# A hybrid attention layer on one core: the opening's transfers in order of use on one queue, and idle products fed from a constant

## The chip, the cores and the metric

The kernel runs on one core of a Trainium2 chip. The metric is device time in microseconds (us) of one execution. The kernel before took 1103.35 us, the median of three runs from 1103.25 to 1103.62.

## What is computed

One layer of a streaming encoder for 256 tokens of width 2048, all in float32:

```python
h = rms_norm(x, attn_norm)                       # x: (1, 256, 2048)
x = x + hybrid_mixer(h, w_in, ..., w_out)        # 8 heads of softmax attention with forget gates,
                                                 # 8 heads of stick-breaking attention
h = rms_norm(x, ffn_norm)
x = x + conv_ffn(h, w_up, conv_w, conv_b, w_down) # up, causal convolution of width 3, gate, down
```

The mixer begins with `proj = h @ w_in`, whose first 512 columns are the queries of four heads. Only the computation of those columns, the opening of the kernel, is touched by the change.

## The kernel before

**Splitting.** Products run on TensorE (PE) in a reduced-precision float32 form. To keep the precision, each operand is split in a high part (a cast) and a low part (the operand less its high part), and high x high, high x low and low x high are added up. So each piece of weights is loaded (`w_raw`), cast on ScalarE (ACT) or VectorE (DVE) to `w_hi`, and subtracted on DVE to `w_lo`; the activations are transposed on PE, scaled with the norm's weights `ga` on ACT to the high part of `hT` (L143) and subtracted on DVE to its low part (L146).

**The opening** (`opening`, L385) makes the first 512 columns. Its 2048 rows of weights are taken in eight chunks c = 0 to 7 of 256 rows (two k-tiles of 128). `load_x(k, n)` (L90) loads n k-tiles of x for both halves of the tokens, on SyncE's queue (SP): 256 KB for n = 2. `load_w(c)` (L391) loads a chunk, 512 KB, and `load_w(c, i)` its half i, 256 KB, by default on SP's queue; in the text w(c,i) and x(k,n). Two chunks share one `w_raw` buffer, and there are three buffers. `columns` (L126) transposes the norm's weights `prow` to `ga`. `split_w(c)` (L402) makes a chunk's high and low parts; for chunk 0 it also transposes x(0,2), and for chunk 1 it casts the two halves on DVE (L415) and transposes x(2,2). `multiply(c, i, n, high)` (L423) makes the products of a chunk: with `w_hi`, per k-tile two with the high and two with the low part of `hT`, one for each half of the tokens; with `w_lo`, two with the high part. `behind(c)` (L454) puts the transposes and splits of later chunks ahead of a chunk's products. `sums_of_squares` (L155) runs on ACT.

**What sets the order.** The opening is written with the order of PE, DVE, ACT and SP fixed by hand: each engine executes its instructions as they stand in the code. A transfer is issued by an instruction of SP or ACT, in that engine's order; the two have a queue each (q1 and q10 in the profile), and both feed the same 16 DMA engines. A scheduler gives each transfer one of eight semaphores in turn, so a transfer can wait for an earlier one's landing. The order of the issues before is L433 to L448: on SP x(0,2), w(0,0), x(2,2), w(1,1), x(4,2), w(2), x(6,2), w(3), and so on; on ACT the norm's weights, then, behind the load of the activation table, w(0,1) and w(1,0).

**Idle products.** While the first transfers are on the way, PE has nothing to do. `keep_busy(n)` (L379) puts n products of 128x128 by 128x256 bfloat16 in its order, whose result nobody reads: 14 ahead of `columns`, 4 behind the transposes of chunk 0. They read `zeros`, a tile that DVE fills at L371. The preamble of every program fills some constants on GpSimd (L1160), among them a bfloat16 1.0 in each partition.

Behind the opening stand the rest of the projection, the attention heads, the output projection and the feed-forward part. The order on PE is fixed by hand there too, and weights are loaded up to six steps ahead.

Of the kernel before, what the change touches and what calls it, by code (L numbers as in the profile page):

```python
# [14 lines left out]
P = 128  # L15
D = 2048
S = 256
NT = S // P
KT = D // P
# [26 lines left out]
def hybrid_layer(  # L46
# [19 lines left out]
    nc = tc.nc  # L66
    act, dve = nc.scalar, nc.vector
# [10 lines left out]
    def f32(t):  # L78
        return t.bitcast(F32)
# [4 lines left out]
    prow = const.tile([50, P], F32, name="prow")  # L84
# [5 lines left out]
    def load_x(k, n):  # L90
        nc.sync.dma_start(x2[:, :, k * P : (k + n) * P], xp[:, :, k * P : (k + n) * P])
# [29 lines left out]
    ga = const.tile([P, KT], F32, name="ga")  # L121
# [4 lines left out]
    def columns(dst, rows, n):  # L126
        pp = psb.tile([P, 512], F32, name="pp", tag="t")
        nc.tensor.transpose(pp[:, :n], rows, ident[:n, :n])
        dve.tensor_copy(dst, pp[:, :n])
# [3 lines left out]
    def transposed_split(k, g, n=2):  # L133

        ps = psb.tile([P, 2, S], F32, name="ps_x", tag="t")
        for j in range(n):
            for t in range(NT):
                nc.tensor.transpose(  # L138
                    ps[:, j, t * P : (t + 1) * P], xt[t][:, (k + j) * P : (k + j + 1) * P], ident
                )  # L140
        for j in range(n):
            i = k + j
            act.activation(hT[:, i, 0, :], ps[:, j, :], AF.Identity, scale=g[:, i : i + 1])  # L143
        for j in range(n):
            i = k + j
            dve.scalar_tensor_tensor(  # L146
                hT[:, i, 1, :], ps[:, j, :], g[:, i : i + 1], f32(hT[:, i, 0, :]),
                op0=ALU.mult, op1=ALU.subtract,
            )

    def sums_of_squares(ss, c, tiles=range(NT)):

        for t in tiles:
            junk = late.tile([P, 512], F32, name="junk", tag="raw", bufs=4)
            act.activation(junk, xt[t][:, c * 512 : (c + 1) * 512], AF.Square, accum_out=ss[:, t, c : c + 1])  # L155
# [62 lines left out]
    def rows_of(w, k0, n, c0, cols):  # L218
        return w[k0 * P : (k0 + n) * P, c0 : c0 + cols].rearrange("(k p) c -> p k c", p=P)
# [14 lines left out]
    def of_half(h, part, t):  # L234
        return h[:, part, t * P : (t + 1) * P]
# [51 lines left out]
    with ExitStack() as actx:  # L287

        at = actx.enter_context(tc.tile_pool(name="at", bufs=1))
# [77 lines left out]

        zeros = at.tile([P, S], mybir.dt.bfloat16, name="zeros")  # L370
        dve.memset(zeros, 0.0)  # L371
        nc.gpsimd.memset(ident, 0.0)
        nc.gpsimd.affine_select(
            ident, ident, pattern=[[-1, P]], base=0, channel_multiplier=1,
# [2 lines left out]
        idle = pss.tile([P, S], F32, name="idle", tag="s")  # L377

        def keep_busy(n):  # L379
            for _ in range(n):  # L380
                nc.tensor.matmul(idle, zeros[:, :P], zeros, start=True, stop=True)

        ss1 = const.tile([P, NT, 4], F32, name="ss1")

        def opening():  # L385

            acc = psa.tile([P, NT, 512], F32, name="acc", tag="acc")
            pairs = [[(0, 1), (1, 1)]] + [[(0, 2)]] * 7
            raws, parts = [], []

            def load_w(c, which=None, queue=nc.sync):  # L391

                if c == len(raws):
                    raw = wraw.tile([P, 2048], F32, name="w_raw", tag="w_raw")
                    raws.extend([raw[:, :1024], raw[:, 1024:]])
                for i, n in [(which, 1)] if which is not None else [(0, 2)]:
                    queue.dma_start(
                        raws[c][:, i * 512 : (i + n) * 512].rearrange("p (a b) -> p a b", a=n),
                        rows_of(wi, 2 * c + i, n, 0, 512),
                    )  # L400

            def split_w(c):  # L402
                hi = whi.tile([P, 2048], F32R, name="w_hi", tag="w_hi")
                lo = wlo.tile([P, 2048], F32R, name="w_lo", tag="w_lo")
                parts.append([t[:, :1024].rearrange("p (a b) -> p a b", a=2) for t in (hi, lo)])
                for i, n in pairs[c]:
                    cols = slice(i * 512, (i + n) * 512)
                    if c == i == 0:
                        dve.tensor_copy(hi[:, cols], raws[c][:, cols])
                        for k in range(2):  # L410
                            transposed_split(k, ga, 1)
                    elif c == 1:
                        for j in range(2):
                            half = slice(512 * j, 512 * (j + 1))
                            dve.tensor_copy(hi[:, half], raws[c][:, half])  # L415
                        transposed_split(2, ga)
                    else:
                        act.copy(hi[:, cols], raws[c][:, cols])
                    dve.tensor_tensor(
                        lo[:, cols], raws[c][:, cols], f32(hi[:, cols]), op=ALU.subtract  # L420
                    )

            def multiply(c, i, n, high):  # L423
                hi, lo = (p[:, i : i + n] for p in parts[c])
                order = [(j, l, hi) for j in range(n) for l in range(2)] if high else [(j, 0, lo) for j in range(n)]
                for m, (j, l, r) in enumerate(order):
                    for t in range(NT):
                        nc.tensor.matmul(  # L428
                            acc[:, t, :], of_half(hT[:, 2 * c + i + j], l, t), r[:, j, :],
                            start=high and c == i == m == 0, stop=not high and c == 7 and m == n - 1,  # L430
                        )

            load_x(0, 2)  # L433
            nc.scalar.dma_start(prow[:KT, :], attn_norm[0].rearrange("(n p) -> n p", p=P))
            act.preload_act_table_set("natural_log_exp_and_others")
            load_w(0, 0)
            load_w(0, 1, nc.scalar)
            load_x(2, 2)
            load_w(1, 0, nc.scalar)
            load_w(1, 1)  # L440
            load_x(4, 2)
            load_w(2)
            load_x(6, 2)
            load_w(3)
            load_x(8, 4)
            load_w(4)
            load_x(12, 4)
            load_w(5)  # L448
            keep_busy(14)
            columns(ga, prow[:KT, :], KT)  # L450
            split_w(0)
            keep_busy(4)

            def behind(c):  # L454
                if c:
                    transposed_split(2 * c + 2, ga)
                split_w(c + 1)

            multiply(0, 0, 1, True)
            multiply(0, 1, 1, True)  # L460
            behind(0)
            sums_of_squares(ss1, 0, [0])
            multiply(0, 0, 1, False)
            multiply(0, 1, 1, False)
            for c in range(1, 8):
                if c < 7:
                    behind(c)
                sums_of_squares(ss1, c // 2, [c % 2])
                if c == 2:
                    load_w(6)  # L470
                    load_w(7)
                multiply(c, 0, 2, True)
                multiply(c, 0, 2, False)
            return acc

        with tc.high_priority(offset=AHEAD), tc.manual_schedule(
            engines={mybir.EngineType.PE, mybir.EngineType.DVE, mybir.EngineType.Activation, mybir.EngineType.SP}
        ):
            acc_q0 = opening()
# [301 lines left out]
        for group in range(2):  # L781
# [3 lines left out]
            for c in range(4):  # L785
# [7 lines left out]
                if c == 0:  # L793
                    pg = psb.tile([P, NT], F32, name="pg", tag="t")
                    for t in range(NT):
                        nc.tensor.matmul(
                            pg[:, t : t + 1], ssq[group][:, t * P : (t + 1) * P], ones[:, 0:1],
                            start=t == 0, stop=t == NT - 1,
# [376 lines left out]
```

## Time and profile before

| | |
|---|---|
| runs, median (lowest to highest) | 1103.35 us (1103.25 to 1103.62) |
| the profiled execution | 1103.81 us |
| span, first to last instruction | 1102.0 us |
| busy: PE, DVE, ACT, GpSimd | 1096.5, 877.7, 701.9, 44.4 us |
| HBM read | 242.82 MB, 222 GB/s over the span |
| packets on q1 (SP), share of 16 DMA engines | 162458, 58.6% |
| packets on q10 (ACT), share | 320, 0.1% |

The profile is one execution, recorded by the hardware. PE are the matrix products, PEld the loads of their stationary operand, SPq and ACTq the issues of transfers by SP and ACT. A row of the timeline gives start and length in us, engine, line of the kernel, operation, what is written from what, shapes and count; in brackets how long the engine stood idle before it and what ended that. A chain of waits follows the end back to what each step waited for. "Landing" is when all of a transfer's bytes have been reported.

### The profile page before, as it was taken

What the parts mean: (1) busy time and instruction counts of PE and PEld (TensorE: products, weight loads), DVE (VectorE), ACT (ScalarE), POOL (GpSimd) and SP (SyncE); (2) the same over time, 40 slices, a digit from 0 to 9 for tenths busy, and PEclk for the clock granted to TensorE, in tenths of its full rate; (3) what the DMA queues carried; (4) which work ended last, traced back from release to release, by engine and by line L of the source; (5) the groups of instructions that cost most, each with busy time, mean ns of one, the idle gap of its engine ahead of it and who ended that gap; (6) DMA issues with size and microseconds to landing.
All of it is one profiled execution on the core that took longest, in us unless ns stands there. A gap on an engine that the chain in (4) does not pass through costs nothing.

```text
span 1102.0 us, 14826 instructions
## 1 busy us (share of the span) xinstructions
PE 1096.5 (99%) x5868; PEld 951.2 (86%) x5868; DVE 877.7 (80%) x941; ACT 701.9 (64%) x879; POOL 44.4 (4%) x46
## 2 busy tenths in 40 slices
PE   9999999999999999999999999999999999999998
PEld 7998888888888888888888888888888888888887
DVE  5655777975775677689889988889798889889896
ACT  6544556664653566677767776767676777677753
POOL 0000000000000000000000010100000010100010
PEclk9999999999999999999999999999999999999999
DMA  8776654576545396558989597986979689997985
GB/s 288 171 244 230 188 156 153 153 231 197 184 161 186 112 317 196 181 191 209 288 223 312 191 234 264 261 269 177 315 209 303 217 218 282 241 266 198 322 208 177
DMA packets 179407, 245.89 MB, mean 223 GB/s; under 512 B 4432, under 2 KB 119018, under 8 KB 179082
## 3 DMA queue, kind: packets, MB, share of 16 engines
q1 hardware_dynamic: 162458, 209.67, 58.6%
q0 software_dynamic: 16560, 34.75, 16.8%
q8 instruction: 46, 0.75, 0.3%
q10 hardware_dynamic: 320, 0.53, 0.1%
q14 instruction: 23, 0.19, 0.0%
HBM read 242.82 MB, written 2.11 MB: 222 GB/s over the span
## 4 chain that ended last, share of the span: by engine, by line
PE 99%; DMA 0%; DVE 0%; SPq 0%; issue 0%
PE pu L254 34%; PE acc L229 22%; PE pu L260 18%; PE bank_a L229 10%; PE bank_b L229 5%; PE bank_c L229 2%; PE acc L428 2%; PE acc L1053 1%; PE ps_x L138 1%; PE ps_o L593 1%; PE bank_a L1053 1%; PE ps_p L607 0%; DMA w_raw<-in_w_in_dram 0%; PE ps_o L594 0%; PE ps_h L307 0%; PE ps_s L522 0%
## 5 line engine op out<-in xcount | busy, mean ns | idle before, releaser
L208 DVE TENSOR_TENSOR w_lo<-w_raw,w_hi 128x2048 fp32r<-128x2048 f32 (+1 forms) x196 | 439.6, 2246 | 129.5 <-ACT w_hi L207 128.6
L207 ACT CAST w_hi<-w_raw 128x2048 fp32r<-128x2048 f32 (+1 forms) x196 | 367.3, 1877 | 235.9 <-PE acc L229 66.6
L254 PE MATMUL pu<-hT,w_hi 128*128 128x512 f32 x1664 | 394.0, 390 | 0.0
L254 PEld LDWEIGHTS pu<-hT,w_hi 128*128 128x128 f32 x1664 | 310.3, 188 | 63.2
L260 PEld LDWEIGHTS pu<-hT,w_lo 128*128 128x128 f32 x1664 | 211.9, 191 | 7.0
L260 PE MATMUL pu<-hT,w_lo 128*128 128x256 f32 x1664 | 215.1, 283 | 0.0
L229 PE MATMUL acc<-w_hi,hT 128*128 128x512 f32 (+1 forms) x576 | 124.5, 368 | 0.0
L229 PEld LDWEIGHTS acc<-w_hi,hT 128*128 128x128 f32 x576 | 101.5, 188 | 14.3
L207 ACT CAST w_hi<-w_sum 128x2048 fp32r<-128x2048 f32 x30 | 57.3, 1909 | 44.2 <-PE pu L254 36.6
L208 DVE TENSOR_TENSOR w_lo<-w_sum,w_hi 128x2048 fp32r<-128x2048 f32 x30 | 68.7, 2290 | 20.8 <-ACT w_hi L207 20.7
L870 ACT ACTIVATE tap<-up,ccol 128x256 f32<-128x256 f32 x176 | 74.6, 495 | 0.0
L229 PE MATMUL acc<-w_lo,hT 128*128 128x512 f32 (+1 forms) x288 | 64.6, 366 | 0.0
L229 PEld LDWEIGHTS acc<-w_lo,hT 128*128 128x128 f32 x288 | 51.6, 188 | 7.5
L975 POOL DMA_DIRECT2D w_sum<-in_w_down_dram x20 | 25.7, 1284 | 797.7 <-DVE w_lo L208 786.1
L229 PE MATMUL acc<-w_hi,oT 128*128 128x512 f32 x192 | 46.0, 392 | 0.0
L229 PEld LDWEIGHTS acc<-w_hi,oT 128*128 128x128 f32 x192 | 35.7, 188 | 7.3
L229 PE MATMUL bank_a<-w_hi,g 128*128 128x512 f32 x160 | 40.0, 392 | 0.0
L229 PE MATMUL bank_b<-w_hi,s 128*128 128x512 f32 x160 | 40.0, 392 | 0.0
L229 PE MATMUL bank_a<-w_hi,s 128*128 128x512 f32 x160 | 40.0, 392 | 0.0
L229 PEld LDWEIGHTS bank_b<-w_hi,s 128*128 128x128 f32 x160 | 28.9, 189 | 5.2
L229 PEld LDWEIGHTS bank_a<-w_hi,g 128*128 128x128 f32 x160 | 28.8, 189 | 5.3
L229 PEld LDWEIGHTS bank_a<-w_hi,s 128*128 128x128 f32 x160 | 28.9, 189 | 5.2
(211 smaller groups left out, 1068.7 us busy)
## 6 DMA issues: line engine op xcount, KB each, us to landing
w_raw<-in_w_up_dram SPq DMA_DIRECT2D x88, 1024.0 KB, 7.5
w_raw<-in_w_down_dram SPq DMA_DIRECT2D x44, 1024.0 KB, 6.4
w_raw<-in_w_in_dram SPq DMA_DIRECT2D x36, 1024.0 KB, 5.4
w_sum<-in_w_down_dram POOLq DMA_DIRECT2D x20, 1024.0 KB, 9.9
w_raw<-in_w_out_dram SPq DMA_DIRECT2D x16, 1024.0 KB, 5.1
w_raw<-in_w_down_dram POOLq DMA_DIRECT2D x10, 1024.0 KB, 14.9
w_raw<-in_w_in_dram SPq DMA_DIRECT2D x12, 688.0 KB, 4.2
w_raw<-in_w_in_dram SPq DMA_DIRECT2D x6, 512.0 KB, 6.8
```

Source lines behind the costliest of these rows:

```text
L138: nc.tensor.transpose(ps[:, j, t * P : (t + 1) * P], xt[t][:, (k + j) * P : (k + j + 1) * P], ident)
L207: act.copy(hi[:, :n], raw[:, :n])
L208: dve.tensor_tensor(lo[:, :n], raw[:, :n], f32(hi[:, :n]), op=ALU.subtract)
L229: nc.tensor.matmul(o, lhs(i, l, t), r[:, i, :], start=starts and j == 0, stop=stops and j == 3 * n - 1, skip_group_check=more,)
L254: nc.tensor.matmul(acc[:, j, :], hi[:, i, j * P : (j + 1) * P], hT[:, k].rearrange("p a b -> p (a b)"), start=k == 0, stop=low_first and k ...
L260: nc.tensor.matmul(acc[:, j, S:], lo[:, i, j * P : (j + 1) * P], hT[:, k, 0, :], start=False, stop=not low_first and k == KT - 1,)
L428: nc.tensor.matmul(acc[:, t, :], of_half(hT[:, 2 * c + i + j], l, t), r[:, j, :], start=high and c == i == m == 0, stop=not high and c == ...
L593: nc.tensor.matmul(po, v[j][:, hs], wp[:, k], start=i == 0, stop=False)
L870: act.activation(taps[w][:, j, :], u[:, j, w : w + S], AF.Copy, scale=ccol[:, w, f : f + 1])
L975: nc.gpsimd.dma_start(mem[into][:, : nk * 512].rearrange("p (a b) -> p a b", a=nk), src, accum_op=ALU.add)
L1053: nc.tensor.matmul(o, of_half(g, l, t), r[:, i, c0 : c0 + cols], start=kh == 0 and j == 0, stop=kh == n - 1 and j == 11,)
```

## The change

The tile `zeros` and its memset go; the idle products read a view `some` of the preamble's 1.0, each partition's one element repeated (step 0). On SP's queue stand x and the first weights in the order in which they are used: x(0,2), w(0,0), w(0,1), x(2,2), w(1,0), x(4,2), w(1,1), x(6,2). ACT issues the norm's weights at the start, as before, and no longer w(0,1) and w(1,0); w(2) is now issued by ACT, and stands there behind the splitting of chunk 0 (two activations of L143 and a cast of L418). The other loads keep their order on SP. There are 16 idle products ahead of `columns`, for 14, and 3 behind the transposes of chunk 0, for 4.

```diff
-        zeros = at.tile([P, S], mybir.dt.bfloat16, name="zeros")
-        dve.memset(zeros, 0.0)
+        some = nc.const_aps.tensor(1.0, [P, S], mybir.dt.bfloat16)
...
         def keep_busy(n):
             for _ in range(n):
-                nc.tensor.matmul(idle, zeros[:, :P], zeros, start=True, stop=True)
+                nc.tensor.matmul(idle, some[:, :P], some, start=True, stop=True)
...
-            load_x(0, 2)
             nc.scalar.dma_start(prow[:KT, :], attn_norm[0].rearrange("(n p) -> n p", p=P))
             act.preload_act_table_set("natural_log_exp_and_others")
+            load_x(0, 2)
             load_w(0, 0)
-            load_w(0, 1, nc.scalar)
+            load_w(0, 1)
             load_x(2, 2)
-            load_w(1, 0, nc.scalar)
+            load_w(1, 0)
+            load_x(4, 2)
             load_w(1, 1)
-            load_x(4, 2)
-            load_w(2)
             load_x(6, 2)
+            keep_busy(16)
+            columns(ga, prow[:KT, :], KT)
+            split_w(0)
+            keep_busy(3)
+            load_w(2, queue=nc.scalar)
             load_w(3)
             load_x(8, 4)
             load_w(4)
             load_x(12, 4)
             load_w(5)
-            keep_busy(14)
-            columns(ga, prow[:KT, :], KT)
-            split_w(0)
-            keep_busy(4)
```

## The prediction

> **What bounds the kernel now.** I read the page's busy shares first, then the waits of PE, then the chain of work that ended last over the first 14 us, and last the instructions of that stretch one by one. The page has (busy us and share of the span, then the chain's shares):
>
> ```profile
> PE 1096.5 (99%) x5868; PEld 951.2 (86%) x5868; DVE 877.7 (80%) x941; ACT 701.9 (64%) x879; POOL 44.4 (4%) x46
> ...
> PE 99%; DMA 0%; DVE 0%; SPq 0%; issue 0%
> ```
>
> PE is busy for 1096.5 of 1102.0 us, and the chain is PE for 99%. The waits of PE (who waited for what, total us, times, longest) say where it was not busy:
>
> ```profile
> PE idle L381 <- DVE zeros L371: 1.1, 1, 1.1
> PE acc L428 <- DVE w_hi L409: 1.1, 1, 1.1
> PE ps_x L138 <- DMA x<-in_x_dram: 0.2, 1, 0.2
> ```
>
> All three lie in the first 7 us. After that PE doesn't wait, so what the opening gains or loses is carried unchanged to the end, and nothing that happens to other engines counts unless it makes PE wait. The chain's beginning (start, length, what):
>
> ```profile
> 0.74 0.43 SPq L91
> ...
> 1.23 4.77 DMA w_raw<-in_w_in_dram
> ...
> 6.02 0.44 DVE w_hi L409
> 6.46 0.14 issue
> 6.59 2.06 PE acc L428 x8
> 8.66 0.44 PE ps_x L138 x4
> ...
> 10.03 0.44 PE ps_x L138 x4
> ```
>
> The first half tile of weights, w(0,0) from here on, is issued at 1.23 and lands at 6.00; a cast of 0.44 and a semaphore of 0.14 later the first real product starts at 6.59. That transfer is the bound of the opening. How a gain there would travel on is read in the timeline (start, length, engine, line, tiles):
>
> ```profile
> 1.06 3.04 PE L381 MATMUL idle<-zeros 128*128 128x256 bf16 x14 [1.06 <-DVE zeros L371]
> 1.22 1.28 ACT L435 ACT_TABLE_LOAD   x1 [1.22 <-PEq L1160]
> 1.25 0.94 ACTq L397 DMA_DIRECT2D w_raw<-in_w_in_dram  x2
> ...
> 4.45 0.66 PE L138 MATMUL ps_x<-cs,x 128*128 128x128 f32 x4 [0.20 <-DMA x<-in_x_dram]
> ...
> 4.93 0.84 ACT L143 ACTIVATE hT<-ps_x,ga 128x256 fp32r<-128x256 f32 x2 [2.42 <-PE ps_x L138]
> 4.95 0.60 PE L381 MATMUL idle<-zeros 128*128 128x256 bf16 x4
> ...
> 6.24 0.62 ACT L418 CAST w_hi<-w_raw 128x512 fp32r<-128x512 f32 x1 [0.48 <-DMA w_raw<-in_w_in_dram]
> ...
> 8.35 0.76 DVE L415 CAST w_hi<-w_raw 128x512 fp32r<-128x512 f32 x2
> ...
> 10.00 0.88 DVE L146 SCALAR_TENSOR_TENSOR hT<-ps_x,ga,hT 128x256 fp32r<-128x256 f32 x2 [0.90 <-ACT hT L143]
> ...
> 10.80 1.21 DVE L419 TENSOR_TENSOR w_lo<-w_raw,w_hi 128x1024 fp32r<-128x1024 f32 x1
> 11.24 1.05 ACT L418 CAST w_hi<-w_raw 128x1024 fp32r<-128x1024 f32 x1
> ...
> 12.16 1.10 PE L428 MATMUL acc<-w_lo,hT 128*128 128x512 f32 x4
> ...
> 13.46 2.09 PE L428 MATMUL acc<-w_hi,hT 128*128 128x512 f32 x8
> ```
>
> The point to watch is 12.16, the low products of chunk 1: they wait for a chain on DVE (the two casts of chunk 1, the two low halves of hT, the low weights) that takes 12.16 - 10.00 = 2.16 us from the hT step on. From 13.46 on each chunk is PE after PE.
>
> **The transfers.** Two views. First the bytes by stretch (stretch, its length, five engines, clock, DMA share, GB/s); then, in two fences, packets and MB of the queues (q1 is SP's, q10 ACT's), from 0 to 3 us and from 3 to 7 us.
>
> ```profile
> 0.00:3.00 3.00, 1.94 (x10) 1.40 (x11) 0.17 (x1) 1.28 (x1) 1.09 (x8) 1.00 0.33 75
> 3.00:4.00 1.00, 1.00 (x6) 0.56 (x4) 0.00 (x0) 0.00 (x0) 0.00 (x0) 1.00 0.92 250
> 4.00:5.00 1.00, 0.80 (x7) 0.67 (x7) 0.17 (x1) 0.07 (x1) 0.00 (x0) 1.00 1.05 322
> 5.00:6.00 1.00, 0.55 (x6) 0.24 (x3) 0.00 (x0) 0.77 (x2) 0.00 (x0) 1.00 0.93 292
> 6.00:7.00 1.00, 0.41 (x2) 0.39 (x3) 0.98 (x3) 0.62 (x1) 0.00 (x0) 1.00 1.02 343
> 7.00:8.00 1.00, 1.00 (x6) 0.84 (x5) 1.00 (x3) 0.00 (x0) 0.00 (x0) 1.00 1.01 353
> 8.00:9.00 1.00, 1.00 (x8) 0.83 (x8) 1.00 (x3) 0.00 (x0) 0.00 (x0) 1.00 1.07 405
> ```
>
> ```profile
> q10 hardware_dynamic: 29, 0.01, 1.8%
> ```
>
> ```profile
> q1 hardware_dynamic: 530, 0.69, 60.2%
> q10 hardware_dynamic: 287, 0.52, 38.1%
> ```
>
> Added up, 0.23 MB have moved by 3 us, 0.48 by 4, 0.80 by 5, 1.09 by 6, 1.43 by 7, 1.79 by 8, 2.19 by 9. The engines are 92 to 107% busy from 3 us on, so what ACT's queue moves, SP's can't. Now x(0,2), w(0,0) and w(0,1), 0.80 MB with the norm's rows, have all passed by about 5.0, and they are seen at 6.00 and 6.24: a landing lies 1.0 to 1.25 us behind the bytes. x(0,2) fits: 0.27 MB at 3.2, used at 4.45. I take 1.1.
>
> **The change, part by part.**
>
> *Order of use on SP's queue.* The first seven transfers, 0.26 MB each behind 0.01, come one after the other: x(0,2), w(0,0), w(0,1), x(2,2), w(1,0), x(4,2), w(1,1). If the same bytes move in the same time, they have passed at 3.2, 4.2, 5.0, 5.9, 6.7, 7.4 and 8.1, and land at 4.3, 5.3, 6.1, 7.0, 7.8, 8.5 and 9.2. SP issues one in about 0.49 (0.74 to 1.23), the last of the seven near 3.9, ahead of its bytes by 3 us: that costs nothing. Bounds for w(0,0): 4.2 + 1.0 if SP's queue takes all that ACT's had, and 6.00 as now if one queue alone doesn't fill the engines; I take 5.3, as the engines were busy with SP's queue almost alone before 4 us.
>
> First product: 5.3 + 0.44 + 0.14 = 5.9, 0.7 earlier. The fifth product needs w(0,1): 6.1 + 0.62 + 0.14 = 6.85; the first eight start 2.06/8 = 0.26 apart, so now it starts near 7.6. **Gain up to here 0.7.** The transposes of x(2,2) then want to start at 8.66 - 0.7 = 8.0 (landed 7.0), those of x(4,2) at 9.3 (landed 8.5): no wait.
>
> *What is late next: w(1,1).* It goes from sixth to seventh place and lands at 9.2. Its cast takes 0.4, and DVE, in order, does the hT step only behind it: 9.6, where ACT's hT would allow 10.00 - 0.7 = 9.3. The low products start at 9.6 + 2.16 = 11.8 instead of 12.16. **Gain left: 0.35.** At both ends of the lag: 0.25 to 0.45. If w(1,1) were no hindrance, 0.7.
>
> *w(2) from ACT's queue.* On SP it is issued ninth, at 3.91. On ACT it stands behind two activations and the cast of w(0,1). Sequencer work runs ahead of the engine (ACT issued two transfers at 1.25 under its table load of 1.28), but not past an instruction that waits: so it goes when w(0,1) lands, at about 6.1. Behind it on ACT stand the hT activations of chunk 1, due near 8.4; the issue, 0.94/2 = 0.47, is hidden. When its bytes start I bound by two rows: 1.0 us after the issue (x(0,2), issued at 0.74, has moved most of its bytes by 3), or 2 us (ACT's issues at 1.25 had moved 0.01 MB by 3.0). I take the second, as SP's backlog stands ahead here too: start 8.1, when w(1,1) has passed. With half of some 390 GB/s its 0.52 MB take 2.7: passed at 10.8, landed at 11.9, cast by 12.95, ready at 13.1. The high products of chunk 2 want 13.46 - 0.35 = 13.1. It just fits; I give 0.05 for it.
>
> *The constant in place of zeros.* The memset and PE's wait for it (1.06) go; the products can start near 0.8, as ACT and SP start at 0.74. Sixteen products at 3.04/14 = 0.22 end at 4.3 at the latest, less once the clock rises; then the columns of the norm, ga, and the first hT by about 5.3, before the cast of w(0,0) at 5.7. Worth nothing and costing nothing as long as they end before 4.6. That three follow instead of four saves 0.15 on PE while it waits anyway.
>
> *Order of the other issues.* w(3) and what follows it stays in SP's order, with one transfer fewer ahead; nothing is late there.
>
> **Sum:** 0.35 - 0.05 = 0.3 less. The profiled execution took 1103.81 (span 1102.0 and 1.8 around it), 0.46 above the runs' median of 1103.35. It would give 1103.5, and the median 1103.05.
>
> **The rivals.**
>
> *1. w(2) overtakes w(1,1).* If ACT's bytes start 1 us after the issue, at 7.15, about 1.49 MB have passed and 0.35 MB stand before the end of w(1,1). From 3 to 7 us q10 moved 0.52 of 1.21 MB, though it had work for only part of that time: two queues with work share about evenly. At half of 380 GB/s the 0.35 MB take 1.85: passed 9.0, landed 10.1, hT step 10.5, low products 12.65: 0.5 **slower**, 1103.85. It decides from a landing of w(1,1) after 9.6 on. The Trainium skill, "DMA: Bandwidth & Descriptors", section "Queues, rings and completion order", says that each engine goes round the queues that have work, packet by packet; by that rule and an early start this rival holds, and the trace's shares agree with it.
>
> *2. w(2) is late.* Eight transfers can be under way; the ninth waits for an early one:
>
> ```profile
> 3.91 0.38 SPq L397 DMA_DIRECT2D w_raw<-in_w_in_dram  x1
> ...
> 4.43 0.66 SPq L91 DMA_DIRECT2D x<-in_x_dram  x1
> ```
>
> ```profile
> SPq L397 <- DMA prow<-in_attn_norm_dram: 0.5, 1, 0.5
> ```
>
> In written order w(2) is tenth and waits for x(0,2), long landed. If the scheduler gives it a later place, it waits for x(4,2) or w(1,1) and is issued at 8.5 to 9.2, or for w(3) at about 12.5. ACT waits with it, and so do hT of chunk 1 and all behind. An unhindered load lands in 4.1:
>
> ```profile
> w_raw<-in_w_in_dram SPq DMA_DIRECT2D x6, 688.0 KB, 4.1
> ```
>
> So w(2) lands at 12.6 to 16.6, and chunk 2 starts 1.15 later, at 13.75 to 17.75 against 13.46: 0.3 to 4.3 slower, 1103.65 to 1107.65. It decides from a landing after 12.3 on.
>
> *3. The first bytes don't come earlier.* If one queue leaves the engines idle in the gaps, w(0,0) lands near 6.0 and nothing moves: 1103.35 or up to 0.1 beside it. Against it: at 8 to 9 us SP's queue alone moved 405 GB/s.
>
> *4. The clock.* The first fourteen idle products run 0.22 apart (3.04/14), the four at 4.95 at most 0.15 (0.60 with the tail of the last): TensorE became faster by a factor of 1.45 or more between them, within 3.9 us of its start. If in the changed kernel that came only after the start of the real products, the slow rate for 3.04 us of them would cost 3.04 x 0.45 = 1.4 or more: 1104.45 with the gain taken off. Starting at 0.8 rather than 1.06, with two more products in the first row, speaks against it; one product fewer in the second speaks for it. The Trainium skill, "TensorE: Matmul & The Clock Gate", Part 1, puts the rise at the end of a free-running window of about 3.4 us with enough work in it; the trace's rise within 3.9 us agrees, and where the window stands in a run no row here shows.
>
> **How the numbers follow.** The forecast (0.1 to 0.75 faster) gets 0.50, rival 1 0.25, rival 3 0.10, rival 2 0.11, rival 4 0.04. The likeliest is 1103.05. The range reaches down to the gain of 0.7 with the runs' own spread and the lead at the start (1.1 in all), up over rival 1 and the nearer part of rival 2: 1102.2 to 1104.5, which leaves out the far part of rival 2, part of rival 4 and what I have not thought of, some 1 to 2 in 10. 0.2%, 2.2 us, is about what a measurement of this kernel can tell from no change; only the far end of rival 2 gets there on the slow side, and on the fast side nothing worked out here does, as the first product can't precede x(0,2) at 4.45 and its transposes. Faster 0.02, same 0.92, slower 0.06.
>
> **What would show it.** First idle product near 0.8 with no DVE ahead of it; the cast of w(0,0) near 5.3 and the first real product near 5.9; the second cast of chunk 1 near 9.2, the low products of chunk 1 near 11.8; ACT's issue of w(2) near 6.1, q10 empty before 8. A second cast after 9.6 means rival 1; PE waiting for chunk 2's cast means rival 2; a first product at 6.5 means rival 3. The prediction is wrong if PE's order or its waits change after 14 us.

## The result and the profile after

| | before | after |
|---|---|---|
| median (lowest to highest) | 1103.3 us (1103.15 to 1103.62, 4 runs) | 1114.1 us (1113.88 to 1114.79, 4 runs) |
| the profiled execution; its span | 1103.81; 1102.0 us | 1114.79; 1113.0 us |

The change makes the kernel 1.0% slower: ratio 1.0099, 95% interval 1.0083 to 1.0114, where 1103.05 us and no measurable difference were forecast. The page of after, in the places shown of before (busy us, then the chain's shares):

```profile
PE 1100.5 (99%) x5869; PEld 953.0 (86%) x5869; DVE 879.1 (79%) x940; ACT 702.9 (63%) x879; POOL 44.4 (4%) x46
...
PE 98%; DMA 2%; ACT 0%; SPq 0%; issue 0%; DVE 0%; ACTq 0%
```

PE is still 99% busy, but 2% of the chain are now transfers, where there were none. The waits of PE (who waited for what, total us, times, longest):

```profile
PE pu L254 <- ACT w_hi L207: 5.3, 1, 5.3
PE acc L427 <- ACT w_hi L417: 3.2, 2, 2.5
...
```

The longest wait is not in the opening at all: L254 is the up-projection of the feed-forward part. I matched each product of PE with the same product of before. After runs 3.4 us behind from 17 to 380 us, and 11.0 us behind from 410 us to the end, and neither distance grows within its stretch. So there are two losses.

**First loss, the opening.** The timeline of after:

```profile
0.78 3.57 PE L380 MATMUL idle<-const-bfloat16-1.0 128*128 128x256 bf16 x16 [0.78 <-PEq L1159]
...
4.68 0.97 SPq L396 DMA_DIRECT2D w_raw<-in_w_in_dram  x1
...
5.69 0.69 SPq L91 DMA_DIRECT2D x<-in_x_dram  x1
...
5.74 1.25 PE L427 MATMUL acc<-w_hi,hT 128*128 128x512 f32 x4
...
6.96 0.62 ACT L417 CAST w_hi<-w_raw 128x512 fp32r<-128x512 f32 x1 [0.88 <-DMA w_raw<-in_w_in_dram]
...
7.63 1.20 PE L427 MATMUL acc<-w_hi,hT 128*128 128x512 f32 x4 [0.64 <-ACT w_hi L417]
...
7.77 0.40 ACTq L396 DMA_DIRECT2D w_raw<-in_w_in_dram  x1
...
12.63 1.19 PE L427 MATMUL acc<-w_lo,hT 128*128 128x512 f32 x4
...
15.69 1.05 ACT L417 CAST w_hi<-w_raw 128x1024 fp32r<-128x1024 f32 x1 [4.18 <-DMA w_raw<-in_w_in_dram]
16.79 2.14 PE L427 MATMUL acc<-w_hi,hT 128*128 128x512 f32 x8 [2.53 <-ACT w_hi L417]
```

The first real product starts at 5.74, before at 6.59. But the fifth, on w(0,1), starts at 7.63 (before 7.58), the low products of chunk 1 at 12.63 (before 12.16), and chunk 2 at 16.79 (before 13.46): 3.3 us late, because w(2) landed at 15.6. ACT issued it at 7.77. What moved meanwhile, the packets and MB of the queues tell, first from 7 to 11 us, then from 11 to 14 us:

```profile
q1 hardware_dynamic: 1024, 1.47, 104.1%
```

```profile
q1 hardware_dynamic: 363, 0.65, 59.1%
q10 hardware_dynamic: 255, 0.50, 45.3%
```

From 7 to 11 us nothing of ACT's queue (q10) moved; the first packet of w(2) follows at 11.4. SP's queue moved nearly all of x(6,2), w(3) (issued at 4.68) and x(8,4) (5.69) first, the last two 1.05 MB, all issued before 7.77.

**Second loss, the way into the feed-forward part.** The chain of waits around 390 to 410 us (start, length, what), of before and of after:

```profile
389.58 5.46 PE acc L229 x24
395.03 1.81 PE pu L254 x8
396.85 0.95 PE pu L260 x8
```

```profile
392.96 3.66 PE acc L229 x16
...
396.63 5.06 DMA w_raw<-in_w_up_dram
...
401.79 1.91 ACT w_hi L207
...
403.74 3.78 PE pu L254 x8
407.52 1.29 PE pu L260 x8
```

Before, the last products of the output projection (acc) run on into the up-projection (pu). After, between them lie the load of the first up-weights, which only begins when the 16th product is done, and its cast: PE stands still from 398.41 to 403.74, 5.33 us. Behind that the same products take 3.78 and 1.29 in place of 1.81 and 0.95: 2.3 more. The next rows say why (stretch, length, five engines, then granted clock, DMA share, GB/s):

```profile
401.00:404.00 3.00, 0.26 (x1) 0.26 (x2) 1.49 (x8) 2.31 (x3) 0.00 (x0) 0.56 1.09 349
404.00:408.00 4.00, 4.00 (x12) 3.23 (x13) 3.35 (x2) 2.16 (x2) 0.00 (x0) 0.50 1.09 348
408.00:412.00 4.00, 4.00 (x28) 3.68 (x28) 3.24 (x2) 1.66 (x1) 0.00 (x0) 0.98 1.09 348
```

The granted clock is half up to 408. Opening 3.4, wait 5.33 and half clock 2.3 are the 11.0 us between the spans. Who held the load back, the waits of SP's queue from 340 to 420 us name, in before and in after:

```profile
SPq L200 <- DVE w_lo L208: 55.6, 10, 13.4
```

```profile
SPq L200 <- PE acc L229: 7.0, 1, 7.0
```

After, one load waits 7.0 us for products of the output projection, which has nothing to do with the up-weights.

**Theory.** SBUF is laid out by pools, and a tile that goes moves all that stands behind it. In the built programs the four `w_raw` buffers of the feed-forward part take bytes 121888 to 154656 of each partition, in both kernels. The pool of the attention part's high weights (`whi`) stands behind the tile `zeros` of 512 bytes: it begins at 154912 before and at 154400 after. So with the tile there is a gap of 256 bytes between the two, and without it an overlap of 256, and the first load into those buffers must wait until the output projection has read its last high weights. That first load itself goes to bytes 121888 to 130080, outside the overlap: in the built programs its wait is for a product of PE in after and for a step of DVE in before, so the wait belongs to the four buffers as a whole. The change thus touches more than the opening. The opening's loss is w(2)'s place in the order of issue. **Rivals:** the constant or the new order of the opening does the late damage by timing; w(2) is late because it is on ACT's queue, and not because of when it is issued.

### The profile page after: what moved, and what is told of

It is laid out like the page before. It is cut to its first block, busy times and chain, and to the rows that moved or that the text cites. A ratio compares the mean times of both kernels' runs of the same rounds, so it can differ in the third digit from the quotient of the medians.

```text
span 1113.0 us, 14826 instructions
## 1 busy us (share of the span) xinstructions
PE 1100.5 (99%) x5869; PEld 953.0 (86%) x5869; DVE 879.1 (79%) x940; ACT 702.9 (63%) x879; POOL 44.4 (4%) x46
## 4 chain that ended last, share of the span: by engine, by line
PE 98%; DMA 2%; ACT 0%; SPq 0%; issue 0%; DVE 0%; ACTq 0%
PE pu L254 34%; PE acc L229 22%; PE pu L260 18%; PE bank_a L229 10%; PE bank_b L229 5%; PE bank_c L229 2%; PE acc L427 2%; PE acc L1052 1%; DMA w_raw<-in_w_in_dram 1%; PE ps_o L592 1%; PE bank_a L1052 1%; DMA x<-in_x_dram 0%; PE ps_p L606 0%; PE ps_x L138 0%; DMA w_raw<-in_w_up_dram 0%; PE ps_o L593 0%
## 5 line engine op out<-in xcount | busy, mean ns | idle before, releaser
L254 PE MATMUL pu<-hT,w_hi 128*128 128x512 f32 x1664 | 395.8, 391 | 5.3 <-ACT w_hi L207 5.3
L254 PEld LDWEIGHTS pu<-hT,w_hi 128*128 128x128 f32 x1664 | 311.2, 189 | 69.1 <-ACT w_hi L207 5.7
## 6 DMA issues: line engine op xcount, KB each, us to landing
w_sum<-in_w_down_dram POOLq DMA_DIRECT2D x20, 1024.0 KB, 10.2
```

The costliest lines, as they stand in the source:

```text
L254: nc.tensor.matmul(acc[:, j, :], hi[:, i, j * P : (j + 1) * P], hT[:, k].rearrange("p a b -> p (a b)"), start=k == 0, stop=low_first and k ...
```

## The experiments

The kernel before took 1103.36 to 1103.47 us beside those that were timed. Each diff is against after, unless it says otherwise.

**1. The tile kept, not read.**

```diff
+        zeros = at.tile([P, S], mybir.dt.bfloat16, name="zeros")
+        dve.memset(zeros, 0.0)
         some = nc.const_aps.tensor(1.0, [P, S], mybir.dt.bfloat16)
```

> The changed kernel with the 512-byte tile of zeros and its memset put back, but unread: the idle products still read the constant. Theory 1 (addresses): without that tile everything behind it in its pool lies 512 bytes lower, and the feed-forward part's first weight buffers (end at byte 154656 of a partition) run 256 bytes into the old high-weight buffers (from 154400; with the tile from 154912). Then the wait of 5.3 us before the up-projection and the half clock behind it go: 1114.1 - 5.3 - 2.4 = 1106.4, and the 3.3 us lost in the opening stay. Rival (order): the wait comes from the new order of transfers and semaphores in the opening, carried along; then 1114.

Measured 1106.92 us (1105.8 to 1108.77), ratio 1.0033 (1.0022 to 1.0044). The chain:

```profile
391.80 5.46 PE acc L229 x24
397.25 1.81 PE pu L254 x8
399.06 0.95 PE pu L260 x8
```

The wait is gone, with the half clock behind it: the tile alone, which nobody reads, is worth 7.2 us. The opening's loss is still there (chunk 2 at 15.64).

**2. The other way round: before, with the constant in place of the tile and nothing else.**

> The kernel before with only its idle products reading the constant, and without the tile of zeros; order and counts of the opening as before. Theory 1 (addresses): the wait before the up-projection and the half clock appear, 1103.3 + 7.7 = 1111.0, with an opening as before. Rival (order): 1103.3.

Measured 1110.97 us (1110.39 to 1111.83), ratio 1.0069 (1.0054 to 1.0084). The opening's order is that of before, and the chain has the wait:

```profile
388.98 3.66 PE acc L229 x16
...
392.65 5.01 DMA w_raw<-in_w_up_dram
...
397.76 1.91 ACT w_hi L207
...
399.71 3.74 PE pu L254 x8
```

So it isn't the opening's timing.

**3. The constant, with the tile kept, in before.**

> The kernel before with the idle products reading the constant, and the tile and its memset kept unread: the constant without its consequence for addresses. First idle product at 0.78 instead of 1.06. Theory: it lies beside the wait for transfers, so nothing measurable: 1103.2 to 1103.5.

Measured 1103.46 us (1103.11 to 1105.49), ratio 1.0001 (0.9992 to 1.001). Reading the constant is worth nothing, as forecast; what cost was that the tile went.

**4. How many bytes matter.** The tile with 256 bytes of a partition (`at.tile([P, P], ...)`; `whi` begins at 154656, exactly where the feed-forward part's buffers end) and with 224 (`[P, P - 16]`, an overlap of 32 bytes), one execution each:

> The changed kernel with a tile of 256 bytes in the place of the 512 of before: the old high-weight buffers then begin at byte 154656, just where the feed-forward part's weight buffers end. Theory (addresses): no overlap, no wait before the up-projection, clock at full speed, some 1106.5 to 1107. Rival (any shift of the pool will do it, or the wait needs the full 512 bytes): 1114.

> The same with a tile of 224 bytes: the old buffers begin at 154624, an overlap of 32 bytes. Theory (addresses): the wait of 5.3 us and the half clock are back, 1114. Rival (the overlap counts by its size): between 1107 and 1108.

They took 1108.8 and 1119.28 us. With 256 bytes there is no wait before the up-projection; with 224 it is back, 5.35 us long, and so is SP's, though the memset stands in both:

```profile
SPq L200 <- PE acc L229: 7.0, 1, 7.0
```

That is the theory's borderline to the 32 bytes. The built programs agree: the first up-load waits for a product of PE without the tile (after, experiment 2) and with 224 bytes, and for a step of DVE with 256, 480 and 512. But 1119.28 is 5 us more than expected. Matched product by product, 3.3 of them go between 50 and 380 us, on products that wait for nothing, and another 2 us late, from 1060 us on. So I tried 480 bytes, which moves the pools behind the tile by 32 bytes without an overlap, and 256 once more:

> The changed kernel with a tile of 480 bytes of a partition in the place of the old one of 512, filled and not read by the idle products. Everything behind it in the attention part's pools lies 32 bytes lower than with the whole tile; the high weights of that part begin at 154880, 224 bytes behind the end of the up-projection's weight buffers (154656). Theory (the wait before the up-projection comes from an overlap of these two, and from nothing else that the tile does): no wait before the up-projection, and the last products of the output projection run on into it at full clock. The look at 224 bytes lost 3.4 us more between 50 and 380 us, on PE products with no wait between them; if that comes from a shift that is no multiple of 64 bytes, it is here too, and the time is that of the kernel with the whole tile and some 3.4 more: 1110.3 (1109.5 to 1111). If it was a single execution's accident, 1106.9 (1106 to 1108). Rival to the addresses (any tile smaller than 512 bytes brings the wait back): 1113 to 1115 or more.

> The kernel with a tile of 256 bytes, once more and timed. Its high weights begin at 154656, where the up-projection's weight buffers end: no overlap, no wait before the up-projection, no slower products between 50 and 380 us (a shift of 256 is a multiple of 64): 1106.9 (1106 to 1108). The first look gave 1108.8, of which 0.7 was lost at once near 70 us and 1.7 lay in a later chunk 2; if these belong to the layout and not to that execution, the time is 1108.5 to 1109.

Measured 1110.7 us (1110.1 to 1111.66), ratio 1.0067 (1.0052 to 1.0082), and 1107.1 us (1106.25 to 1108.77), ratio 1.0033 (1.002 to 1.0045). Neither waits before the up-projection. With 480 bytes, the 3.3 us between 50 and 380 us are there again, so they belong to the shift by 32 bytes: products from 50 to 380 us, by shape (count, busy us, mean ns of one), in experiment 1 with the whole tile, then with 480 bytes:

```profile
L229 PE MATMUL acc<-w_hi,hT 128*128 128x512 f32 x353 | 85.1, 393 | 0.0
L254 PE MATMUL pu<-hT,w_hi 128*128 128x512 f32 x256 | 60.8, 391 | 0.0
L229 PE MATMUL acc<-w_lo,hT 128*128 128x512 f32 x176 | 43.5, 389 | 0.0
L229 PE MATMUL acc<-w_hi,oT 128*128 128x512 f32 x176 | 42.2, 392 | 0.0
```

```profile
L229 PE MATMUL acc<-w_hi,hT 128*128 128x512 f32 x352 | 86.4, 397 | 0.0
L254 PE MATMUL pu<-hT,w_hi 128*128 128x512 f32 x256 | 62.0, 396 | 0.0
L229 PE MATMUL acc<-w_lo,hT 128*128 128x512 f32 x176 | 44.6, 395 | 0.0
L229 PE MATMUL acc<-w_hi,oT 128*128 128x512 f32 x172 | 41.3, 392 | 0.0
```

The first three are 1 to 1.5% longer, the fourth is not. In the built programs the weights `w_hi` and `w_lo` and the tiles `oT` move by the 32 bytes, and `hT` stays where it was: the products that got longer pair a tile that moved with one that didn't. Not every such product did: those of `hT` and `w_lo` with 256 columns went from 284 to 280 ns. Shifts of 512 (after) and 256 bytes leave the first three at 392, 391 and 389. Why a shift by 32 bytes counts stays open, and so do the 2 us from 1060 us on, which only the one execution at 224 bytes had.

**5. PE kept busy through the wait.** After, with 22 idle products of 512 columns between the two projections:

```diff
+    busy = psf.tile([P, 512], F32, name="busy", tag="a")
+    some = nc.const_aps.tensor(1.0, [P, 512], mybir.dt.bfloat16)
+    for _ in range(22):
+        nc.tensor.matmul(busy, some[:, :P], some, start=True, stop=True)
```

> The changed kernel with 22 idle products of 512 columns (some 4.7 us) on PE between the output projection and the up-projection. The wait for the weights stays. Theory: the half clock of 6.8 us there comes from PE standing idle, so it goes, and 2.3 us with it: 1111.8. Rival: the clock falls whatever PE does, or its fall costs nothing that counts: 1114.

Measured 1112.67 us (1112.05 to 1114.49), ratio 1.0086 (1.0071 to 1.0101). The clock stays full though the weights still come late, so the half clock comes from PE standing idle. But only 1.4 of the 2.3 us come back, and the chain says where the rest went:

```profile
395.53 5.13 DMA w_raw<-in_w_up_dram
...
400.75 1.91 ACT w_hi L207
...
402.69 2.30 DVE w_lo L208
...
405.03 1.22 PE pu L260 x8
```

At full clock PE gets through the high products before DVE has the low weights: the late load makes both parts late, and the half clock had covered some of that. My expectation had missed it.

**6. w(2) on SP, in the place of use.** Experiment 1 with w(2) taken off ACT:

```diff
             load_w(1, 1)
+            load_w(2)
             load_x(6, 2)
...
-            load_w(2, queue=nc.scalar)
```

> The first kernel of this list with w(2) on SP's queue, ahead of x(6,2), where it is used: the order of use alone. Theory 1: chunk 2 does not wait; the opening ends within 0.5 us of before, 1102.9 to 1103.8. The prediction's own step (w(0,0) earlier, w(1,1) later) gives 1103.05. Rival: if the loss of 3.3 us came from one queue being slower than two, chunk 2 starts after 14.5 and the time is over 1104.5.

Measured 1104.11 us (1103.69 to 1105.47), ratio 1.0005 (0.9995 to 1.0014): 2.8 less than experiment 1. The order of use alone, which is the change without its two losses, gains nothing that shows. Its timeline:

```profile
5.54 1.25 PE L429 MATMUL acc<-w_hi,hT 128*128 128x512 f32 x4
...
7.92 1.19 PE L429 MATMUL acc<-w_hi,hT 128*128 128x512 f32 x4 [1.12 <-ACT w_hi L419]
...
12.59 1.12 PE L429 MATMUL acc<-w_lo,hT 128*128 128x512 f32 x4
...
13.90 2.10 PE L429 MATMUL acc<-w_hi,hT 128*128 128x512 f32 x8
```

The first product comes 1.05 earlier than before, waits 1.12 for w(0,1) four products later, and chunk 2 starts at 13.90 for 13.46.

**7. The queue or the order of issue.** Experiment 1 with w(2) on SP, but issued where it stands in after's order, behind w(3) and x(8,4) (`first=2` only lets w(3) open the buffer that it shares with w(2)):

```diff
-            load_w(2, queue=nc.scalar)
-            load_w(3)
+            load_w(3, first=2)
             load_x(8, 4)
+            load_w(2)
```

> The tile kept, and w(2) on SP's queue, but behind w(3) and x(8,4): the same order of issue as in the changed kernel, on one queue. Theory (order of issue): w(2) lands at 14 to 15.5 as there, chunk 2 starts at 15.3 to 16.7 and the time is that of the changed kernel with the tile kept, 1106.9. Rival (ACT's queue or ACT's wait is the cause): chunk 2 starts before 14.5, 1104.

Measured 1106.67 us (1105.86 to 1108.76), ratio 1.0031 (1.0019 to 1.0043), as experiment 1 (1106.92). w(2) is issued at 6.30, and

```profile
14.26 1.04 ACT L419 CAST w_hi<-w_raw 128x1024 fp32r<-128x1024 f32 x1 [3.29 <-DMA w_raw<-in_w_in_dram]
15.35 2.63 PE L429 MATMUL acc<-w_hi,hT 128*128 128x512 f32 x8 [1.91 <-ACT w_hi L419]
```

It lands 7.9 us after its issue on SP's queue, as it does on ACT's in after (15.6 - 7.77 = 7.8). The order of issue makes it late; the choice of the queue makes no difference that shows.

**8. The two loads put behind w(2) on ACT.** Experiment 1 with w(3) and x(8,4) on ACT's queue too, behind w(2).

> The changed kernel with the tile kept, and with w(3) and x(8,4) on ACT's queue too, behind w(2): ACT still issues w(2) near 7.2 us. Theory: transfers are served in the order of their issue over both queues; w(2) was late because w(3) and x(8,4), 1.05 MB, had been issued ahead of it on SP. Then its bytes follow x(6,2), it lands near 11.5 to 12 and chunk 2 starts at 13.3 to 13.9, as with w(2) on SP: 1103.5 to 1104.5. Rival: ACT's queue, or an issue as late as 7.2, is itself too slow: landing after 14, chunk 2 after 15, 1106 or more.

Measured 1109.55 us (1109.38 to 1110.11), ratio 1.0056 (1.0042 to 1.0069): a miss, and no answer to its question. The scheduler's turn of semaphores changed; w(2) got that of x(6,2), which landed at 10.12:

```profile
10.14 0.91 ACTq L398 DMA_DIRECT2D w_raw<-in_w_in_dram  x2
...
12.14 0.73 PE L429 MATMUL acc<-w_hi,hT 128*128 128x512 f32 x2 [2.09 <-ACT hT L143]
```

ACT stood at that issue until 10.14, with the hT of chunk 1 behind it, and PE waited 2.09 for them. This is rival 2 of the prediction at work.

**9. Before, with w(0,1) and w(1,0) on SP, in the same order of issue.**

```diff
-            load_w(0, 1, nc.scalar)
+            load_w(0, 1)
+            load_w(1, 0)
             load_x(2, 2)
-            load_w(1, 0, nc.scalar)
```

> The kernel before with w(0,1) and w(1,0) on SP's queue in the place that their issue times gave them: x(0,2), w(0,0), w(0,1), w(1,0), x(2,2), w(1,1), x(4,2). Only the number of queues differs. Theory (two queues keep the engines fuller than one in the first 8 us: 1.79 MB by 8 us before, 1.61 in the changed kernel): w(1,1) and x(4,2) land 0.5 to 1 us later, 1103.9 to 1104.3. Rival (order made e3's loss): 1103.4.

Measured 1103.99 us (1103.67 to 1105.99), ratio 1.0006 (0.9997 to 1.0016). One queue seems some 0.5 us worse than two, but the interval takes in no change. Its first product starts at 5.32 and its fifth waits 0.93, as in experiment 6: with one queue w(0,0) landed at 4.6 and 4.7 for 6.0 before, w(0,1) at 6.8 and 7.2 for 6.2.

## Why the prediction was wrong

*"Nothing that happens to other engines counts unless it makes PE wait", "carried unchanged to the end"; "worth nothing and costing nothing".* **This is the step that failed most.** It took the profile of before, in which PE doesn't wait after 7 us, for the profile of after, and looked at what the memset does and not at where its tile lies. The wait for the memset was worth nothing (experiment 3); the 512 bytes were worth 7.2 us (experiment 1), or 7.5 without the rest of the change (experiment 2). No rival had it. Its own test, that PE's waits after 14 us don't change, found it at once. Its length adds up from after's rows: a load that starts only when the last reader is done costs its 5.06 and the cast's 1.91, less the 1.8 of the products still to run.

*w(2), issued at about 6.1, bytes from 8.1, "ready at 13.1", at 0.05.* This is the step that failed in the opening. Measured were 7.77, 11.4 and 16.74. The issue came late because it waits for the landing of x(2,2) (7.74), whose semaphore it shares, and not only for that of w(0,1) (6.93 for 6.1): in experiment 1 w(0,1) landed at 5.79 and x(2,2) at 7.15, and ACT issued w(2) at 7.17. The bytes came late because the prediction counted SP's backlog only as far as w(1,1): x(6,2), w(3) and x(8,4) were issued ahead of w(2) as well, though the code writes two of them behind it. "Nothing is late there", on the order of the other issues, is the same slip: with ACT waiting for a landing, what SP issues meanwhile is ahead. Rival 2 had the end (chunk 2 between 13.75 and 17.75) from one of the two mechanisms, the semaphore, with a chance of 0.11; but it had an issue at 8.5 or later and a load of 4.1, where 7.77 and 7.8 were measured. Experiments 6 and 7 show the order of issue as the cause.

*"Gain up to here 0.7."* The first product came near its forecast (5.74 for 5.9), but by luck: w(0,0) landed at 4.70 for 5.3, and what came last was hT, whose transposes ran from 4.49 at half clock. At the fifth, which the prediction allowed from 6.85 on, the gain was gone (7.63, before 7.58), since w(0,1) landed 0.8 later than worked out. In the other executions with this opening the fifth started at 7.24 to 7.44, in experiment 1 at 6.49.

*"If the same bytes move in the same time."* From 0 to 8 us (last column GB/s), before and then after:

```profile
0.00:8.00 8.00, 5.69 (x29) 4.10 (x30) 2.32 (x7) 2.74 (x4) 1.09 (x8) 1.00 0.74 223
```

```profile
0.00:8.00 8.00, 6.59 (x30) 4.30 (x31) 2.52 (x8) 2.76 (x4) 1.09 (x8) 1.00 0.67 201
```

One queue moved 1.61 MB, two 1.79. w(1,1) landed at 10.2 for 9.2, and the low products of chunk 1 started at 12.63 for 11.8: a gain of 0.35 became a loss of 0.5. Experiment 6 has the same 12.59, and six more executions with after's opening have 12.06 to 13.02. Two queues moved 1.90 and 1.88 MB in experiments 2 and 3, one queue 1.59 to 1.71 in the others; only experiment 8, with less issued on SP, had 1.79 with one. So one queue tended to move less, but the number of queues isn't shown to be the whole cause. And w(0,1), ahead of x(2,2) in the new order, was already issued 0.02 behind w(0,0) in before: what was to be put in order was nearly in order.

*Rival 1, an even share.* It did not come about, though its sign, a second cast of chunk 1 after 9.6, did (10.23), and its 12.65 for the low products was met (12.63): w(1,1) was late before a byte of w(2) had moved. The rule of the Trainium skill ("DMA: Bandwidth & Descriptors", "Queues, rings and completion order"), that an engine goes round the queues that have work, would have given w(2) part of the engines while x(6,2) to x(8,4) moved; here q10 moved nothing from the issue at 7.77 to 11.4, and a load on SP's own queue took as long (experiment 7). From 11 to 14 us both queues moved, 0.65 and 0.50 MB, as the rule has it. In these runs the order of issue decided, over both queues, when a load's bytes began; why, no run shows.

*Rival 3* is half of what experiments 6 and 9 show: the time doesn't move, although the first bytes do come earlier. *Rival 4*, the clock in the opening, cost nothing in after: it rose at 5.39 for 3.83 in before, ahead of the first real product at 5.74, and PE then waited 0.64 for w(0,1) anyway. But "within 3.9 us" was one execution. Among the profiles it rose between 3.5 and 6.5, and with one queue the first product went with it: 5.18 to 5.30 where it rose by 3.63 (experiments 1 and 4), 5.90 where it rose at 6.49 (experiment 7).

No version beat before; the best can't be told from it (experiments 3, 6 and 9).

## What to carry to other kernels

A tile that goes, comes or changes its size moves everything that is laid out behind it, so compare the addresses of the two built programs and look for buffers of different stages that newly overlap: there the first load of the later stage waits for the last reader of the earlier one, hundreds of microseconds from the edit. Before moving a load to another engine's queue, list what will have been issued when that engine gets to it, since in these runs nearly all of that went first, and which landing its semaphore waits for. And give the landings that a gain hangs on the spread that executions show: here w(0,1) landed between 5.79 and 6.93 with one and the same opening.

## What the hardware showed beyond that

**When the clock is halved.** In every profile the granted clock changes at whole multiples of 3.413 us after its first rise. I added up PE's idle time in each such window:

| kernel | window, us | idle in it, us | clock after it |
|---|---|---|---|
| before, w(0,1), w(1,0) on SP (9) | 4.15 to 7.56 | 0.93 | full |
| after | 12.21 to 15.63, and 15.63 to 19.04 | 1.37, 1.16 | full |
| w(3), x(8,4) on ACT (8) | 8.36 to 11.77 | 1.71 | full |
| tile kept (1) | 13.87 to 17.29 | 1.76 | full |
| w(2) on SP behind x(8,4) (7) | 13.32 to 16.73 | 1.91 | half, 3.4 us |
| 256 bytes (4), first execution | 12.35 to 15.77 | 2.15 | half, 3.4 us |
| 256 bytes (4), again | 13.75 to 17.16 | 2.31 | half, 3.4 us |
| constant alone (2) | 393.03 to 396.44, and the next | 2.01, 3.27 | half, 6.8 us |
| after | 397.92 to 401.33, and the next | 2.92, 2.41 | half, 6.8 us |

Up to 1.76 us of idle time in one window left the clock full; from 1.91 us on, a little over half of the window, the next one ran at half clock. No other window of the fourteen profiles contradicts this. A wait of 2.53 us in after's opening cost no clock, as it fell on the border of two windows; one of 1.91 in experiment 7 did. Where the windows lie changes from execution to execution, and the spread of the kernels that wait goes with it: in experiment 1 the four runs with a mean clock of 1.000 took 1105.8 to 1106.92 us, the three with 0.998 took 1107.58 to 1108.77. The Trainium skill, "TensorE: Matmul & The Clock Gate", Part 1, has the free-running window of 3413 ns, and the traces agree to 0.01 us; it has the clock go down after an idle window, and here a window idle for 1.9 of 3.4 us was enough.

**32 bytes.** Products of 512 columns that pair weights moved by 32 bytes with `hT`, which stayed, took 396 ns instead of 391, some 3.3 us in this kernel (experiment 4); those of the same weights with `oT`, which moved along, kept their 392, and moves by 256 and 512 cost nothing of the kind.
